# Differential attention heads: two softmax maps combined by the ratio of their sums

## The chip, the cores and the metric

The kernel runs on one core of a Trainium2 chip. The time is the device time of one execution in microseconds (us); before the change the median of three runs is 2071.48 us (2070.87 to 2072.05). The core's engines are called PE (TensorE, matrix products), DVE (VectorE), ACT (ScalarE), POOL (GpSimd) and SP (SyncE, which here only issues DMAs). Each works through its own queue in order and waits on the others by semaphores.

## The reference

One layer of an encoder on a sequence of 16 + 1024 tokens, width 1024, all in float32: a SwiGLU block, a mixing block and a second SwiGLU block, each added to the stream h, and a last norm. In the mixing block the normed stream is projected once, and its columns go to two groups of heads. Four differential heads attend to everything, four pairs of heads of width 64 in a sliding window. The differential part, cut to what is computed:

```python
s = einsum('bqhcd,bkhcd->bhcqk', q, k) * scale      # c = 0, 1: two maps per head
p = softmax(s, axis=-1)
a = p[:, :, 0] - lam * p[:, :, 1]                   # lam: a learned number
o = einsum('bhqk,bkhe->bqhe', a, v)                 # e = 128
o = rmsnorm(o, sub_gain) * (1.0 - lambda_init)      # over e, per head and query; EPS = 1e-6
```

`rmsnorm(x, g)` is `x * rsqrt(mean(x * x) + EPS) * g`. The outputs of both groups go through `w_out` and are added to h.

## The kernel before, in words

The activations lie transposed, features on the 128 partitions and tokens along the row. Large products are made of three float32r products, of a high and a low half of each operand (`split`: ACT casts the high half, DVE or POOL subtracts it for the low one). The kernel is scheduled as a whole: `TileContext(nc, schedule_with_timeline_sim=True)` takes the program's instructions and sets the order of each engine's queue itself, and memory is reused between pools (`Rings`, one pool for each buffer of a ring), with waits where a new buffer lies on an old one. So any edit may change the order in places that it doesn't touch.

The stages by time in the span: the first SwiGLU block, 0 to about 720 us; the projections, 720 to about 1040, with the window attention mixed into their later part; the differential heads, about 1044 to 1320; the second SwiGLU block, to about 1900; the last products and the norm.

Where the projections begin, the first block's last product (`pd`, L167 called from `down_last`) ends, the stream's chunks are normed (`norm_chunk`: `nsq` and `nacc` the squares and their sum, `nps` the sum over partitions on PE, `ns`, `nr` the root, `ny` the normed chunk on DVE L149, `u_hi`, `u_lo` its halves) and `proj_t` (L806) multiplies them with one tile of the input weights after the other. `load_w` loads such a tile into `pwraw` (one buffer), casts `pwhi` on ACT and subtracts `pwlo` on DVE for the first tile, kb, and on POOL for the second, qb. `pj` are the products, `z` what is copied out of them. Behind them `pv` multiplies with the value weights (`wvraw`, `wv_hi`, `wv_lo`).

A differential head has 8 tiles of 128 queries, so there are 32 maps in all. For each, `scores` (L773) makes two score tiles `ds` of 128x1040 on PE (component 0 and 1), DVE takes their row minimum `dmx` (L784; the scores carry a minus sign), and ACT the exponential into `dp0` and `dp1` (L786), with the sum of each row in `z[:, 0]` and `z[:, 1]`, 128x2. `combine` (L789) makes the map of the head: DVE inverts both sums (`drz`), POOL multiplies the second map by its inverse sum and by `neglam` (minus lambda, L793), DVE multiplies the first by its inverse sum and adds (L794). The map is then transposed on PE in blocks of 128x128 (`dt`, L1167, L1175) and copied to `at` by DVE (L1170) and ACT (L1172, L1176); `values` multiplies with v (L1183, `do`) and ACT copies to `oh` (L1186).

The loop over maps works with a lead: at step i the scores of map i, the combine of map i - 1, the transposes of map i - 2 and the values of the pair before. Three maps of the first head are computed early, while the window attention ends (`EARLY`). When a head has four maps, `head_norm` (L1131) squares `oh` on ACT, sums over the partitions by a product with `ones` on PE (`sums`, L1082), takes the root (`rsqrt`, L1095: ACT's table root and one step of refinement on DVE) and scales on POOL (L1122). The next head's keys and queries are loaded and split during the head before (`load_head`, L745; `kl` and the low half of `qst` on POOL, L114 and L760; `kraw` and `qraw` have one buffer each). In the first head the norm of the window part (`win_norm`) uses the same engines, and product tiles of the output weights for it (`out_win`) fill PE's gaps from map 9 on.

Of the kernel before, what the change touches and what calls it, by code (L numbers as in the profile page):

```python
# [10 lines left out]
F32 = mybir.dt.float32  # L11
# [40 lines left out]
def layer(  # L52
# [50 lines left out]
    nc.vector.tensor_scalar(dgain, dgain, -0.5 / P * (1.0 - LAMBDA_INIT), None, op0=ALU.mult)  # L103

    neglam = cpool.tile([P, 1], F32, name="neglam")

    h_d = dpool.tile([D, L], F32, name="h_d")

# [4 lines left out]
    def tt(eng, out, a, b, op):  # L113
        eng.tensor_tensor(out, a, b, op=op)  # L114
# [671 lines left out]
        nc.scalar.activation(p, full, AF.Exp, bias=mx, scale=-1.0, accum_out=z[:, c : c + 1])  # L786
        ps_p.append(p)

    def combine(ps_p, z):  # L789
        rz = dp.tile([P, 2], F32, tag="drz", name="drz")  # L790
        nc.vector.reciprocal(rz, z)
        p0, p1 = ps_p
        nc.gpsimd.tensor_scalar(p1, p1, rz[:, 1:2], neglam, op0=ALU.mult, op1=ALU.mult)  # L793
        nc.vector.scalar_tensor_tensor(p0, p0, rz[:, 0:1], p1, op0=ALU.mult, op1=ALU.add)  # L794
        return p0

    pend, sc = {}, {}
# [1 line left out]
    with ExitStack() as st:  # L799
# [236 lines left out]
        for i, (kv, n) in enumerate(units):  # L1036
# [18 lines left out]
            if i in EARLY:  # L1055
                for t in EARLY[i]:
                    sc[t] = score_tiles()
                    for c in range(2):
                        scores(heads[0], t, c, sc[t], ds0)
                    pend[t] = combine(*sc.pop(t))  # L1060
            if n == NB - 1 and kv == 0:
                for g in range(4):
                    qs[1, g] = win_q(4 + g)
# [9 lines left out]
    with ExitStack() as st:  # L1073
# [5 lines left out]
        ow_hi = op.tile([P, 4, SEQ], F32R, name="ow_hi")  # L1079
        ow_lo = op.tile([P, 4, SEQ], F32R, name="ow_lo")  # L1080

        def sums(srcs, n):  # L1082
            acc = npool.tile([P, 512], F32, tag="nacc", name="nacc")[:, :n]
            for i, s in enumerate(srcs):
                if i == 0:
                    nc.scalar.activation(acc, s, AF.Square)
                else:
                    sq = npool.tile([P, 512], F32, tag="nsq", name="nsq")[:, :n]
                    nc.scalar.activation(sq, s, AF.Square)
                    nc.gpsimd.tensor_tensor(acc, acc, sq, op=ALU.add)  # L1090
            ps = psum.tile([P, 512], F32, tag="do", name="do")[:, :n]
            nc.tensor.matmul(ps, ones, acc, start=True, stop=True)
            return ps

        def rsqrt(v, n, width):  # L1095
            r = npool.tile([P, SEQ], F32, tag="nr", name="nr")[:, :n]
            nc.scalar.activation(r, v, AF.Abs_reciprocal_sqrt, bias=eps, scale=1.0 / width)
            for c0 in range(0, n, 512):
                vc, rc = v[:, c0 : c0 + 512], r[:, c0 : c0 + 512]
                t = npool.tile([P, 512], F32, tag="nt", name="nt")  # L1100
                nc.scalar.activation(t, rc, AF.Square)
                nc.vector.scalar_tensor_tensor(t, vc, EPS * width, t, op0=ALU.add, op1=ALU.mult)
                nc.vector.scalar_tensor_tensor(rc, t, -3.0 * width, rc, op0=ALU.add, op1=ALU.mult)
            return r

# [24 lines left out]

        def head_norm(hd, c, oh):  # L1131
            os = [oh[:, c0 : c0 + n] for c0, n in CH_REAL]
            ps = sums([os[c]], 512)
            if hd == 3:
                head_scale(hd, c, os[c], rsqrt(ps, 512, P))
                return
            if c == 0:
                nvs[hd] = npool.tile([P, SEQ], F32, tag="nv", name="nv")
            nc.scalar.copy(nvs[hd][:, c * 512 : (c + 1) * 512], ps)
            if c == 1:  # L1140
                r = rsqrt(nvs[hd], SEQ, P)
                for j in range(2):
                    head_scale(hd, j, os[j], r[:, j * 512 : (j + 1) * 512])

# [53 lines left out]
        for i in range(NQ + 4):  # L1198
# [6 lines left out]

            def do_combine():
                if N_EARLY < i <= NQ:
                    pend[i - 1] = combine(*sc.pop(i - 1))

            def do_t():  # L1210
                next(tg, None)
# [204 lines left out]
```

## Time and profile before

| | |
|---|---|
| median of the runs | 2071.48 us (2070.87 to 2072.05) |
| the profiled execution's own time | 2074.79 us |
| its span | 2072.9 us |
| mean granted clock of PE | 0.981 of 2.4 GHz |
| PE busy | 1943.9 us, 94% |
| DVE busy | 1279.3 us, 62% |
| ACT busy | 879.4 us, 42% |
| POOL busy | 960.3 us, 46% |

The profile is of one execution; its span runs from the first to the last instruction. Busy time of PE is counted with a pipelined instruction's overlap left out, and a PE at half clock counts as busy too, so busy time and the granted clock are read together.

### The profile page before, as it was taken

The page shows a single profiled execution, that of the slowest core. Times are in us where ns is not written, and L with a number is a line of the kernel's source. Part 1 is how long each engine was busy: PE and PEld are TensorE (multiplying, and loading weights), DVE is VectorE, ACT ScalarE, POOL GpSimd, SP SyncE. Part 2 cuts the span into 40 slices and gives each one's busy share as a digit, 9 for nine tenths or more (in the row PEclk, how much of TensorE's full clock was granted, in tenths as well). Part 3 has the DMA queues.
Part 4 walks back from the last instruction along what each step waited for, and adds up shares of the span by engine and source line. Part 5 has one row for each costly group of instructions (what it writes and reads, how often), then busy time and mean ns, then how long its engine had stood idle before and what let it go on. Part 6 is the DMA issues. An engine that isn't in the chain of part 4 may idle for free.

```text
span 2072.9 us, 30356 instructions
## 1 busy us (share of the span) xinstructions
PE 1943.9 (94%) x11484; PEld 1692.1 (82%) x11484; DVE 1279.3 (62%) x1853; ACT 879.4 (42%) x1611; POOL 960.3 (46%) x807
## 2 busy tenths in 40 slices
PE   5999999998999989899978999898999999989998
PEld 4999999998999879777756777676778888877877
DVE  7855554548875660376766777477665555487745
ACT  6433333334432431366566666354333333344433
POOL 0565454545443740576456432003655554454443
PEclk9999999999999999999988999999999999999999
DMA  5332322328422351544442321622323223375122
GB/s 172 108 109 98 120 92 97 109 92 319 155 64 81 133 174 52 143 122 123 105 113 67 97 85 39 203 102 81 124 106 122 95 89 117 130 282 167 61 82 82
DMA packets 106003, 244.14 MB, mean 118 GB/s; under 512 B 14209, under 2 KB 29009, under 8 KB 105857
## 3 DMA queue, kind: packets, MB, share of 16 engines
q1 hardware_dynamic: 94336, 204.53, 31.1%
q0 software_dynamic: 11520, 37.67, 4.6%
q8 instruction: 90, 1.47, 0.3%
q14 instruction: 57, 0.46, 0.1%
HBM read 169.86 MB, written 65.44 MB: 114 GB/s over the span
## 4 chain that ended last, share of the span: by engine, by line
PE 70%; DVE 11%; DMA 6%; ACT 5%; POOL 3%; issue 3%; SPq 1%; DVEq 0%; POOLq 0%; ACTq 0%
PE p L226 35%; PE pA L577 7%; PE pj L167 5%; PE pC L577 3%; PE pv L884 3%; PE pd L167 2%; PE ds L780 2%; DVE bl L114 2%; PE po L167 2%; PE do L1183 2%; PE pB L577 2%; PE do L167 1%; DMA ru<-wu 1%; POOL s L114 1%; ACT dp L786 1%
## 5 line engine op out<-in xcount | busy, mean ns | idle before, releaser
L114 POOL TENSOR_TENSOR s<-ru 128x512 f32<-128x512 f32 x42 | 55.9, 1331 | 264.5 <-DMA ru<-wu 190.1
L226 PE MATMUL p<-b_hi,wal 128*128 128x260 f32 (+1 forms) x528 | 141.5, 323 | 5.7 <-DVE wal L114 5.7
L226 PE MATMUL p<-b_hi,wah 128*128 128x260 f32 (+1 forms) x528 | 143.2, 325 | 3.6 <-ACT wah L117 1.6
L226 PE MATMUL p<-t_hi,wch 128*128 128x260 f32 (+1 forms) x528 | 141.2, 321 | 5.7 <-DVE u L114 5.7
L226 PE MATMUL p<-b_lo,wah 128*128 128x260 f32 (+1 forms) x528 | 142.5, 322 | 3.4 <-DVE b_lo L114 3.4
L226 PE MATMUL p<-t_lo,wch 128*128 128x260 f32 (+1 forms) x528 | 141.0, 321 | 0.0
L226 PE MATMUL p<-t_hi,wcl 128*128 128x260 f32 (+1 forms) x528 | 140.8, 321 | 0.0
L226 PE MATMUL p<-t_lo,wbh 128*128 128x260 f32 (+1 forms) x504 | 135.5, 319 | 0.0
L226 PE MATMUL p<-t_hi,wbl 128*128 128x260 f32 (+1 forms) x504 | 133.4, 320 | 0.0
L226 PE MATMUL p<-t_hi,wbh 128*128 128x260 f32 (+1 forms) x504 | 133.1, 320 | 0.0
L114 DVE TENSOR_TENSOR u<-p,m 128x520 f32<-128x520 f32 (+1 forms) x88 | 61.0, 693 | 116.5 <-PE p L226 108.9
L117 ACT CAST wbh<-s 128x512 fp32r<-128x512 f32 x84 | 52.1, 621 | 164.9 <-PE p L226 142.1
L577 PE MATMUL pA<-bh,wh 128*128 128x260 f32 (+1 forms) x432 | 115.3, 322 | 2.6 <-DVE h L584 2.6
L577 PE MATMUL pA<-bl,wh 128*128 128x260 f32 (+1 forms) x432 | 114.7, 319 | 0.0
L117 ACT CAST wah<-rg 128x512 fp32r<-128x512 f32 x88 | 53.9, 620 | 143.0 <-PE p L226 112.1
L577 PE MATMUL pA<-bh,wl 128*128 128x260 f32 (+1 forms) x432 | 111.9, 319 | 1.8 <-POOL wl L114 1.8
L114 DVE TENSOR_TENSOR wal<-rg,wah 128x512 fp32r<-128x512 f32 x88 | 74.0, 847 | 63.6 <-ACT wah L117 63.6
L114 DVE TENSOR_TENSOR bl<-r,bh 128x520 fp32r<-128x520 f32 (+1 forms) x126 | 109.0, 900 | 3.3 <-ACT bh L117 2.6
L117 ACT CAST wch<-ru 128x512 fp32r<-128x512 f32 x88 | 54.7, 621 | 130.5 <-PE p L226 72.6
L584 DVE SCALAR_TENSOR_TENSOR h<-pA,h 128x520 f32<-128x520 f32 (+1 forms) x96 | 66.1, 690 | 63.2 <-PE pA L577 63.1
L117 ACT CAST wh<-s 128x384 fp32r<-128x384 f32 x96 | 49.1, 513 | 130.1 <-PE pA L577 65.5
L114 POOL TENSOR_TENSOR s<-wr 128x384 f32<-128x384 f32 x48 | 55.4, 1157 | 100.6 <-DVE wl L114 89.7
(290 smaller groups left out, 6113.2 us busy)
## 6 DMA issues: line engine op xcount, KB each, us to landing
rg<-wg SPq DMA_DIRECT2D x44, 512.0 KB, 3.6
ru<-wu SPq DMA_DIRECT2D x44, 512.0 KB, 5.0
wr<-wd SPq DMA_DIRECT2D x24, 768.0 KB, 4.4
r<-g_t SPq DMA_DIRECT2D x12, 780.0 KB, 5.8
r<-g_t SPq DMA_DIRECT2D x12, 768.0 KB, 5.3
g_b<-g POOLq DMA_DIRECT2D x27, 260.0 KB, 5.2
r<-g_b SPq DMA_DIRECT2D x9, 780.0 KB, 6.4
g_b<-g POOLq DMA_DIRECT2D x27, 256.0 KB, 5.1
```

Source lines behind the costliest of these rows:

```text
L114: eng.tensor_tensor(out, a, b, op=op)
L117: nc.scalar.copy(hi, src)
L167: nc.tensor.matmul(o, w, x[:, c0 : c0 + n], start=first and i == 0, stop=last and i == 2)
L226: nc.tensor.matmul(o, w_k(ww, k), x[:, k, c0 : c0 + cn], start=first and k == 0 and i == 0, stop=k == hk - 1 and i == 2, skip_group_check= ...
L577: nc.tensor.matmul(o, w_k(ww, k), xx[:, c0 : c0 + cn], start=new and k == 0 and q == 0, stop=k == DNG - 1 and q == 2, skip_group_check=not ...
L584: nc.vector.scalar_tensor_tensor(hs, full, 0.5, hs, op0=ALU.mult, op1=ALU.add)
L780: nc.tensor.matmul(o, qs[c][:, qt * P : (qt + 1) * P], kk[:, c0 : c0 + n], start=i == 0, stop=i == 1)
L786: nc.scalar.activation(p, full, AF.Exp, bias=mx, scale=-1.0, accum_out=z[:, c : c + 1])
L884: nc.tensor.matmul(ps[:m, 192 + c * 320 : 512 + c * 320], u[:, k, sl], w[:, k, c * 320 : (c + 1) * 320], start=k == 0 and i == 0, stop=k = ...
L1183: nc.tensor.matmul(po[:, :256], v[:m, j, :], at[:m, j, :], start=j == 0, stop=j == NB)
```

## The change

Softmax's first sum z0 is a factor of a whole row of the combined map, and the norm behind it divides by the row's size anyway. After the change the map stays unnormalised, p0 + p1 * (neglam * z0 / z1), which is z0 times the map of before. The ratio takes two small DVE instructions, a reciprocal of z1 and a scalar_tensor_tensor, both 128x1; one DVE pass of 128x1040 combines, and POOL's pass is gone. The norm's mean of squares is now z0 squared times too large, so its epsilon is multiplied by z0 squared: `combine` stores z0 * z0 of each map in a column of `zsq`, and `sums`, for a head, adds to each block of 128 queries of the squares the diagonal matrix `ident_eps` (EPS * 128 on the diagonal) times that column, four DVE passes of 128x128 for each call, so that the product with `ones` adds it to every row. `rsqrt` then has no epsilon of its own there. `zero`, `zsq` and `ident_eps` are new constants, 644 bytes on each partition, which are allocated ahead of everything else.

```diff
     neglam = cpool.tile([P, 1], F32, name="neglam")
+    zero = cpool.tile([P, 1], F32, name="zero")
+    nc.vector.memset(zero, 0.0)
+    zsq = cpool.tile([P, 4 * NB], F32, name="zsq")
+    ident_eps = cpool.tile([P, P], F32, name="ident_eps")
+    nc.vector.tensor_scalar(ident_eps, ident, EPS * P, None, op0=ALU.mult)
...
-    def combine(ps_p, z):
-        rz = dp.tile([P, 2], F32, tag="drz", name="drz")
-        nc.vector.reciprocal(rz, z)
+    def combine(t, ps_p, z):
+
+        rz = dp.tile([P, 1], F32, tag="drz", name="drz")
+        nc.vector.reciprocal(rz, z[:, 1:2])
+        nc.vector.scalar_tensor_tensor(rz, z[:, 0:1], neglam, rz, op0=ALU.mult, op1=ALU.mult)
         p0, p1 = ps_p
-        nc.gpsimd.tensor_scalar(p1, p1, rz[:, 1:2], neglam, op0=ALU.mult, op1=ALU.mult)
-        nc.vector.scalar_tensor_tensor(p0, p0, rz[:, 0:1], p1, op0=ALU.mult, op1=ALU.add)
+        nc.vector.scalar_tensor_tensor(p0, p1, rz, p0, op0=ALU.mult, op1=ALU.add)
+        tt(nc.vector, zsq[:, t : t + 1], z[:, 0:1], z[:, 0:1], ALU.mult)
         return p0
...
-        def sums(srcs, n):
+        def sums(srcs, n, zs=None):
...
+            for j in range(n // P if zs is not None else 0):
+                aj = acc[:, j * P : (j + 1) * P]
+                nc.vector.scalar_tensor_tensor(aj, ident_eps, zs[:, j : j + 1], aj, op0=ALU.mult, op1=ALU.add)
             ps = psum.tile([P, 512], F32, tag="do", name="do")[:, :n]
             nc.tensor.matmul(ps, ones, acc, start=True, stop=True)
             return ps
 
-        def rsqrt(v, n, width):
+        def rsqrt(v, n, width, e=EPS):
             r = npool.tile([P, SEQ], F32, tag="nr", name="nr")[:, :n]
-            nc.scalar.activation(r, v, AF.Abs_reciprocal_sqrt, bias=eps, scale=1.0 / width)
+            nc.scalar.activation(r, v, AF.Abs_reciprocal_sqrt, bias=eps if e else zero, scale=1.0 / width)
...
-                nc.vector.scalar_tensor_tensor(t, vc, EPS * width, t, op0=ALU.add, op1=ALU.mult)
+                nc.vector.scalar_tensor_tensor(t, vc, e * width, t, op0=ALU.add, op1=ALU.mult)
...
-            ps = sums([os[c]], 512)
+            ps = sums([os[c]], 512, zsq[:, hd * NB + c * 4 : hd * NB + c * 4 + 4])
             if hd == 3:
-                head_scale(hd, c, os[c], rsqrt(ps, 512, P))
+                head_scale(hd, c, os[c], rsqrt(ps, 512, P, 0.0))
```

The scheduler's order changes with it. DVE, where the projections begin: before, the low half of the first projection weight is subtracted ahead of the first block's last operands (`glo`), and waits for its load and for ACT.

```order
L584 SCALAR_TENSOR_TENSOR h_5808<-pA,h_5808 128x520 [waits PE_49]
L114 TENSOR_TENSOR pwlo<-pwraw,pwhi 128x1024 [waits DMAHW6_49,Activation_49]
L584 SCALAR_TENSOR_TENSOR h_5812<-pB,h_5812 128x520 [waits PE_49]
L584 SCALAR_TENSOR_TENSOR h_5808<-pA,h_5808 128x520 [waits PE_49]
L114 TENSOR_TENSOR glo<-graw,ghi 128x1040 [waits DMAHW2_49,Activation_49]
```

After, the same instruction (L119 there) stands some 45 rows further on, in the norm of the second chunk.

```order
L147 SCALAR_TENSOR_TENSOR nr<-ns,nr 128x264 [waits DVE_49]
L154 SCALAR_TENSOR_TENSOR ny<-h_5841,gains,nr 128x264 [waits DVE_49,Pool_49]
L154 SCALAR_TENSOR_TENSOR ny<-h_5833,gains,nr 128x264
L154 SCALAR_TENSOR_TENSOR ny<-h_5825,gains,nr 128x264 [waits Pool_49]
L646 SCALAR_TENSOR_TENSOR h_5821<-pd,h_5821 128x264 [waits PE_49]
L119 TENSOR_TENSOR pwlo<-pwraw,pwhi 128x1024 [waits DMAHW6_49,PE_49]
```

It now waits for PE, and has moved behind the root of the second chunk, three `ny` and an `h`. PE's third projection product, which reads it, has a wait for DVE that it didn't have before.

SP, same place: before, the load of the second projection weight (the second `pwraw` here) stands among the loads of the first block's last operands.

```order
L621 DMA wdraw<-wd 128x512
L175 DMA pwraw<-win 128x1024 [waits DMAHW6_49,PE_49]
L621 DMA wdraw<-wd 128x512 [waits DMAHW3_49,Pool_49]
L621 DMA wdraw<-wd 128x512 [waits DMAHW5_49,DMAHW0_49,Pool_49]
L614 DMA graw<-g_d_102 128x1040 [waits DMAHW1_49,DMASW1_49,DMAHW4_49,DMASW0_49,Pool_49]
L175 DMA pwraw<-win 128x1024 [waits DMAHW6_49,DMAHW2_49,DVE_49]
```

After, it is the first `pwraw` of this piece; the second is the third weight's.

```order
L727 DMA h_d<-h_5821 128x264 [waits DMAHW7_49,DVE_49]
L1161 DMA hrm<-h_d 128x512 [waits DMAHW0_49,PE_49,Activation_49]
L180 DMA pwraw<-win 128x1024 [waits DMAHW1_49,DVE_49]
L1161 DMA hrm<-h_d 128x512 [waits DMAHW2_49]
L727 DMA h_d<-h_5813 128x264 [waits DMAHW3_49,DVE_49]
L180 DMA pwraw<-win 128x1024 [waits DMAHW4_49,DMAHW1_49,Pool_49]
L878 DMA wvraw<-wv 128x640 [waits DMAHW5_49]
```

It has moved behind the stores of h and waits for DVE, which reads the one buffer; the third weight's load, ahead of the value weights, waits for POOL.

POOL, in the first head, where the second head's keys and queries are split: before, the passes of L793 stand in this chain.

```order
L114 TENSOR_TENSOR kl<-kraw,kh 128x1040 [waits DMAHW0_49,DMAHW1_49,PE_49,Activation_49]
L793 TENSOR_SCALAR dp_13143<-dp_13143,drz,neglam 128x1040 [waits DVE_49,Pool_49]
L760 TENSOR_TENSOR qst<-qraw,qst 64x1024 [waits DMAHW4_49,Activation_49,Pool_49]
L793 TENSOR_SCALAR dp_13196<-dp_13196,drz,neglam 128x1040 [waits DVE_49,Pool_49]
L1090 TENSOR_TENSOR nacc<-nacc,nsq 128x512 [waits PE_49,Activation_49]
L114 TENSOR_TENSOR kl<-kraw,kh 128x1040 [waits DMAHW7_49,DMAHW6_49,Activation_49]
```

After:

```order
L119 TENSOR_TENSOR kl<-kraw,kh 128x1040 [waits DMAHW0_49,DMAHW7_49,PE_49,Activation_49]
L765 TENSOR_TENSOR qst<-qraw,qst 64x1024 [waits DMAHW2_49,Activation_49,Pool_49]
L1097 TENSOR_TENSOR nacc<-nacc,nsq 128x512 [waits PE_49,Activation_49,Pool_49]
L119 TENSOR_TENSOR kl<-kraw,kh 128x1040 [waits DMAHW7_49,DMAHW6_49,Activation_49]
L1097 TENSOR_TENSOR nacc<-nacc,nsq 128x512 [waits Activation_49]
```

The query's split follows the key's at once; the rest of the chain keeps its order.

## Rows read from the trace of the kernel before

**Rows 1.** The page: busy time by engine, and the chain that ended last.

```profile
PE 1943.9 (94%) x11484; PEld 1692.1 (82%) x11484; DVE 1279.3 (62%) x1853; ACT 879.4 (42%) x1611; POOL 960.3 (46%) x807
...
PE 70%; DVE 11%; DMA 6%; ACT 5%; POOL 3%; issue 3%; SPq 1%; DVEq 0%; POOLq 0%; ACTq 0%
```

**Rows 2.** Stage windows: length, busy us (instructions) of each engine, PE clock, DMA, GB/s.

```profile
core 0: us, PE busy (x) PEld busy (x) DVE busy (x) ACT busy (x) POOL busy (x), PEclk, DMA share, GB/s
1060.00:1140.00 80.00, 61.35 (x267) 47.62 (x268) 53.35 (x60) 53.12 (x91) 44.16 (x29) 0.81 0.24 67
1140.00:1280.00 140.00, 132.02 (x705) 106.33 (x704) 104.23 (x123) 92.35 (x163) 53.73 (x36) 1.00 0.26 78
```

**Rows 3.** PE's waits, 1140 to 1300: total us, times, longest.

```profile
PE ds L780 <- ACT dp L786: 5.7, 9, 0.9
PE dt L1167 <- ACT at L1176: 5.2, 7, 1.1
```

**Rows 4.** Groups by line, 1044 to 1320: busy us, mean ns | idle before, releaser.

```profile
L794 DVE SCALAR_TENSOR_TENSOR dp<-dp,drz,dp 128x1040 f32<-128x1040 f32 x32 | 43.7, 1365 | 3.4 <-POOL dp L793 3.1
...
L793 POOL TENSOR_SCALAR dp<-dp,drz,neglam 128x1040 f32<-128x1040 f32 x32 | 40.9, 1277 | 75.3 <-DVE drz L791 74.8
...
L1097 ACT ACT_TABLE_LOAD x6 | 7.7, 1283 | 0.1
...
L791 DVE RECIPROCAL drz<-dz 128x2 f32<-128x2 f32 x32 | 5.1, 161 | 18.1 <-ACT dp L786 18.1
```

**Rows 5.** Two single lines of DVE: duration ns min/median/max, when, forms.

```profile
L916 DVE TENSOR_TENSOR neglam<-lsum x1: 160/160/160, 839.2 to 839.2; 128x1 f32<-128x1 f32 x1
...
L913 DVE TENSOR_TENSOR lprod<-lamt x1: 293/293/293, 838.3 to 838.3; 128x128 f32<-128x128 f32 x1
```

**Rows 6.** Timeline of the last head: start us, us, engine, line, instruction [idle before].

```profile
1297.43 1.29 DVE L794 SCALAR_TENSOR_TENSOR dp<-dp,drz,dp 128x1040 f32<-128x1040 f32 x1
...
1307.80 0.66 PE L1167 MATMUL dt<-ident,dp 128*128 128x128 f32 x4 [0.34 <-ACT at L1176]
```

**Rows 7.** Timeline of the projections' start.

```profile
723.25 0.40 PE L167 MATMUL pj<-u_hi,pwlo 128*128 128x512 f32 x1
...
723.92 4.26 DVE L149 SCALAR_TENSOR_TENSOR ny<-h,gains,nr 128x264 f32<-128x264 f32 x3
...
724.40 2.59 POOL L114 TENSOR_TENSOR pwlo<-pwraw,pwhi 128x1024 fp32r<-128x1024 f32 x1
...
726.76 0.40 PE L167 MATMUL pj<-u_hi,pwlo 128*128 128x512 f32 x1
...
728.11 0.42 DVE L641 SCALAR_TENSOR_TENSOR h<-pd,h 128x264 f32<-128x264 f32 x1
...
729.69 1.29 DVE L149 SCALAR_TENSOR_TENSOR ny<-h,gains,nr 128x264 f32<-128x264 f32 x3
...
748.03 1.22 DVE L114 TENSOR_TENSOR pwlo<-pwraw,pwhi 128x1024 fp32r<-128x1024 f32 x1 [2.23 <-ACT pwhi L117]
...
748.99 0.73 PE L167 MATMUL pj<-u_hi,pwhi 128*128 128x512 f32 x2 [1.73 <-ACT z L829]
...
768.66 1.44 PE L884 MATMUL pv<-wv_hi,u_hi 128*128 128x320 f32 x4 [2.99 <-ACT wv_hi L117]
```

**Rows 8.** Timeline of the first head.

```profile
1106.30 1.24 POOL L793 TENSOR_SCALAR dp<-dp,drz,neglam 128x1040 f32<-128x1040 f32 x1
...
1112.46 2.30 DVE L794 SCALAR_TENSOR_TENSOR dp<-dp,drz,dp 128x1040 f32<-128x1040 f32 x1 [1.83 <-POOL dp L793]
...
1116.03 1.04 ACT L759 CAST qst<-qraw 128x1024 fp32r<-128x1024 f32 x1 [1.71 <-DMA qraw<-qa_d]
...
1117.29 1.11 PE L1167 MATMUL dt<-ident,dp 128*128 128x128 f32 x4 [3.08 <-ACT at L1176]
```

**Rows 9.** Window of 8 us around that wait's end, columns as in rows 2.

```profile
1116.00:1124.00 8.00, 6.53 (x22) 4.93 (x22) 2.75 (x4) 4.33 (x9) 7.06 (x5) 0.57 0.53 131
```

**Rows 10.** DMA issues: engine, times, KB each, median us to landing.

```profile
pwraw<-win SPq DMA_DIRECT2D x13, 512.0 KB, 4.5
```

More of the change, by code (lines that the diff above doesn't have):

```diff
@@ L1059, in layer @@
                         scores(heads[0], t, c, sc[t], ds0)
-                    pend[t] = combine(*sc.pop(t))
+                    pend[t] = combine(t, *sc.pop(t))
             if n == NB - 1 and kv == 0:
@@ L1140, in head_norm @@
             if c == 1:
-                r = rsqrt(nvs[hd], SEQ, P)
+                r = rsqrt(nvs[hd], SEQ, P, 0.0)
                 for j in range(2):
@@ L1207, in do_combine @@
                 if N_EARLY < i <= NQ:
-                    pend[i - 1] = combine(*sc.pop(i - 1))
+                    pend[i - 1] = combine(i - 1, *sc.pop(i - 1))
             def do_t():
```

## The prediction

> **What bounds the kernel now.** I read the page's totals first: PE is busy 94% of the span and makes up 70% of the chain that ended last, against 11% for DVE and 3% for POOL [rows 1]. So the change pays only where PE stands still, or runs at half clock, for want of a combined map. Second, the stage windows, to find such places. The differential stage has two halves. In its first head, 1060 to 1140 us, PE is busy 61.35 of 80 us at a granted clock of 0.81; in the steady heads, 1140 to 1280, it is busy 132.02 of 140 at 1.00, and 8.0 us are idle [rows 2]. Third, the waits of PE in the steady heads: none names POOL or the combine; the two large ones are for the exponentials, 5.7 us in 9 waits, and for copies of transposed maps on ACT, 5.2 us in 7 [rows 3]. Last, the timelines of the two places where the order moves: the start of the projections (720 to 770 us) and the first head.
>
> **What the change removes.** 32 POOL passes over 128x1040, mean 1277 ns, and with them the hand-over from POOL to DVE, for which DVE waited 3.1 us in all; the DVE pass behind them keeps its shape, mean 1365 ns [rows 4]. POOL is at 46% and no PE wait of the steady heads is for it, so the 40.9 us themselves are worth nothing.
>
> **What it adds.** Per map on DVE: one 128x1 scalar_tensor_tensor and one 128x1 product, each priced by the 128x1 product at 160 ns, and, as 32 stand in the program for 32 maps, one 128x128 epsilon step, priced by the 128x128 product at 293 ns [rows 5]. The reciprocal gets one column instead of two, at its 161 ns [rows 4]. Sum: 2 x 0.160 + 0.293 = 0.613 us per map, 19.6 us for 32. None of these shapes with a scalar operand from a tile stands in the trace of before; the nearest rows are those two, and from below the bound is nothing where DVE has its idle time. In the steady heads DVE is busy 104.23 of 140 us [rows 2]; some 20 of the 32 maps pass there, so it goes to 116 of 140. From exponential to combined map the path even shortens, by 1.21 for POOL less 0.16 for the ratio; but as PE works two maps behind the scores, nobody waits there. What can come through is a later minimum on DVE, then a later exponential, for which PE does wait. Bounds for the three steady heads: 24 x 0.613 = +14.7 if all of it delays PE, and -5.2 if the waits for copies go. Nearest the rows is almost nothing, as a quarter of DVE is idle: I take +1.5.
>
> In the last head ACT loads its tables twice more, 1283 ns each [rows 4], since the norm's root is put ahead of the last exponential. The last map is combined at 1297.43 + 1.29 = 1298.7, and PE transposes it at 1307.80 [rows 6]: 9.1 us of cover. The two loads, the root and its copy put it off by some 4 us, so the cost is 0, and it would show only if the cover fell under that.
>
> **What the order moves: the start of the projections.** This is the dearest part, and the diff doesn't show it. The low half of the first projection weight (pwlo of kb) was split on DVE long before use; now it stands behind three ny and an h of the norm, since it waits for PE. Before, PE's third projection product, the first that reads it, ran at 723.25 with no wait; three ny begin at 723.92 [rows 7]. At the earliest pwlo now ends at 723.92 + 1.29 (three ny, alone) + 0.42 (h) + 1.22 (a pwlo, alone) = 726.85, which is 3.6 late. At the latest, with the ny as long as they were (4.26) and pwlo as long as on POOL (2.59): 731.19, 7.9 late [rows 7]. What made the three ny 4.26 instead of 1.29 was the other weight's pwlo on POOL from 724.40, and this has moved behind; nacc and u_lo of POOL still stand beside it. I take +5.5, near the middle.
>
> The Trainium skill ("SBUF — State Buffer", section "Who interferes with whom") says that a VectorE instruction with two SBUF inputs and a GpSimd one that reads SBUF exclude each other for a whole instruction. The trace agrees: the excess of 2.97 is even above the 2.59 of the POOL pass beside it. By that rule pwlo, which has two such inputs, waits for what POOL has begun, and the step goes to the 7.9; without it 3.6.
>
> Behind a stall the clock falls: after PE's 3.08 us wait in the first head the granted clock is 0.57 for 8 us, with 6.53 us of PE busy [rows 8, 9], which at full clock would be 3.7; so up to +2.8 more. I take +2. Given back: PE's 1.73 wait for z at 748.99 [rows 7], because kb's last products now come before 24 of the next tile and not right ahead of its successor: -1.7. The second weight is loaded only when the first has been read, say 728.7: its 4.5 us of landing [rows 10] and 2.59 on POOL, with a cast between for which I allow 1, give 736.8. PE meanwhile has 22 products at (726.76 - 723.25)/15 = 0.234 us [rows 7], 5.1, the norm's sums and 16 short ones, some 2.5: 736.3. That is +0.5, with 0 to 2 as bounds. Later PE waits 2.99 for wv_hi [rows 7]; those loads are now queued on SP behind a load that waits for POOL's pwlo, so they slip as well: I count 1 back, bounds 0 to 3. Sum of the place: 5.5 + 2 - 1.7 + 0.5 - 1 = +5.3, from 0 (3.6 - 1.7 + 0 + 0 - 3 and rounded up, since a stall this long hardly vanishes) to +11 (7.9 + 2.8 - 1.7 + 2).
>
> **What the order moves: the first head.** POOL's chain there is key split, map pass, query split, and the query's buffer is single: the pass of 1.24 at 1106.30 stands ahead of the query split, whose end lets the next query load start; ACT waits 1.71 for that load at 1116.03, and PE 3.08 for a copy behind it on ACT; DVE waits 1.83 for POOL and then needs 2.30 instead of 1.29 [rows 8, 4]. In the new order no map pass stands in this chain. The load comes at least 1.24 earlier, at most the whole 3.08 goes: -2.2. The half clock behind it is worth up to 2.8: -2. DVE's 1.83 + 1.01 reaches PE through minimum and exponential, in half I suppose, and other heads of the chain give a little: -1.8. Sum -6. Bounds: the 18.65 us that PE is idle in these 80 [rows 2] from below; +3 from above, if the transposes of the window part, which also change places with the scores, leave one more gap like the 3.08.
>
> The starts of both FFN stages keep their instructions; a few change places at the second, at no price that a row gives: 0, give or take 2.
>
> **Sum.** +5.3 - 6 + 1.5 + 0 = +0.8. On the profiled execution's own 2074.79 that is 2075.6; this one lay 3.3 above the median of the runs shown, 2071.48, and so I forecast 2072 for the median.
>
> **The rivals.**
> 1. Faster: the first head's gaps mostly close, since POOL's and DVE's queues both get lighter there. For it: PE idle 18.65, the clock of 0.81. Against it: most of PE's waits there are for exponentials, whose number is the same. Two thirds of the idle time, -12.4, and with the clock -2.8; with +5.3 at the projections and +1.5: -8.4, that is 2063.
> 2. Slower: the late pwlo stops PE at the projections' start and nothing is given back. Place: PE's third projection product, near 723. It decides once pwlo ends after 729, that is with more than 5.7 of stall: 7.9 + 2.8 - 1.7 + 2 = +11; with the first head at -3 and steady heads at +1.5: +9.5, that is 2081. For it: the wait is now a true dependency, and PE has nothing else in its queue. Against it: the POOL pass that made the ny long has moved away.
> 3. Slower: DVE becomes the bound of the steady heads, at 83% busy. Half of the 14.7 comes through: +7.4, in place of the 1.5: +6.7, that is 2078. Against it: DVE's work is spread evenly, and the longest wait for an exponential is 0.9.
> 4. The change does what it says and both places cost or give under 2 us: 2071 to 2072, told apart from my forecast only by the trace.
>
> **How the numbers follow.** Less than 0.2% (4.1 us) can't be told from no change here. My forecast and rival 4 together: 0.40; rival 1: 0.29; rival 2: 0.22; rival 3: 0.09. Some of rivals 2 and 3 would end within 0.2% and some of my own case outside it, which evens out: faster 0.29, same 0.39, slower 0.32. The likeliest case's own range is 2067.5 to 2076; reaching to rival 1 and rival 2, the range is 2062 to 2083.
>
> **What would show it.** Right at the projections: PE's third product there begins 4 to 8 us after the first, released by DVE's pwlo, with a clock near 0.6 behind it. Right in the first head: PE busy over 61.35 of 80 us or the stretch shorter, no wait of 3 us for a copy. Right in the steady heads: each at most 2 us longer than before, DVE busy 80 to 85%. Wrong: a stage that is longer with its PE waits on DVE's minimum, the norm's sums on PE waiting for the epsilon steps, or a stretch of the FFN that differs by more than 2 us.

## The result: 51 us slower

The changed kernel takes 2122.67 us (2121.17 to 2126.46) against 2071.77 us for the kernel before on the same chip (2070.87 to 2076.78): ratio 1.024, 95% interval 1.0225 to 1.0256. The forecast was 2072 with a range from 2062 to 2083; the time lies 40 us above its end, and no rival came near it.

The page of the changed kernel, busy time and chain, answers to [rows 1]:

```profile
PE 1964.2 (93%) x11484; PEld 1704.3 (80%) x11484; DVE 1296.8 (61%) x1951; ACT 883.0 (42%) x1613; POOL 913.1 (43%) x775
...
PE 73%; DVE 9%; DMA 5%; ACT 5%; POOL 3%; issue 3%; SPq 1%; DVEq 0%; POOLq 0%; ACTq 0%
```

Totals tell little here: DVE has gained 17.5 us, POOL has lost 47.2, PE has the same 11484 products. The profiled span has grown by 48.7 us, so I cut both spans at instructions that both kernels have: the first projection product `pj`, the first score product `ds`, the first product `po` of the output weights with the differential heads, and the start of the last group of `pd` products.

| part | before | after | difference |
|---|---|---|---|
| start to the first `pj` (first feed-forward block) | 722.7 | 728.1 | +5.4 |
| first `pj` to the first `ds` (projections, window attention) | 321.8 | 318.2 | -3.6 |
| first `ds` to the first `po` (differential heads: "the stage" below) | 273.5 | 312.6 | +39.1 |
| first `po` to the last `pd` group (second feed-forward block) | 743.2 | 751.0 | +7.8 |
| rest | 11.7 | 11.7 | 0 |

The stage has four fifths of it. As a whole, before and then after, with the columns of [rows 2]:

```profile
1044.50:1317.90 273.40, 238.05 (x1188) 186.15 (x1186) 185.18 (x217) 173.62 (x303) 116.92 (x76) 0.94 0.29 85
```

```profile
1046.30:1358.90 312.60, 251.36 (x1193) 194.54 (x1191) 212.50 (x314) 176.09 (x306) 74.69 (x46) 0.90 0.26 75
```

PE stands idle 25.9 us longer, and is busy 13.3 us longer with the same products, while the mean granted clock falls from 0.94 to 0.90. In the first head nothing is lost: from the first `ds` to the fourth norm product (`do<-nacc,ones`) it is 107.7 us before and 106.8 after. All of the rest is in the steady heads. Windows of half heads (four maps), each from one norm product to the next, of the kernel before:

```profile
1152.20:1179.00 26.80, 23.91 (x123) 18.18 (x122) 19.61 (x24) 19.11 (x32) 10.18 (x8) 1.00 0.12 41
1179.00:1208.50 29.50, 28.65 (x157) 23.59 (x156) 20.39 (x23) 17.76 (x34) 12.98 (x9) 1.00 0.51 135
...
1237.00:1266.00 29.00, 28.20 (x157) 23.42 (x157) 20.16 (x23) 15.84 (x32) 8.00 (x7) 1.00 0.23 73
```

and of the kernel after; the first line is the first head's window of [rows 2]:

```profile
1060.00:1140.00 80.00, 58.84 (x279) 45.52 (x278) 58.23 (x85) 53.14 (x90) 27.48 (x16) 0.87 0.27 73
...
1153.00:1190.00 37.00, 28.13 (x139) 22.05 (x139) 28.51 (x40) 22.04 (x38) 9.29 (x6) 0.93 0.12 36
1190.00:1224.00 34.00, 31.94 (x152) 25.41 (x153) 22.54 (x36) 16.65 (x31) 5.12 (x3) 0.87 0.44 117
1224.00:1264.00 40.00, 29.50 (x140) 23.11 (x140) 28.51 (x39) 22.36 (x39) 9.56 (x6) 0.91 0.10 33
1264.00:1298.00 34.00, 31.77 (x159) 25.37 (x160) 23.81 (x38) 15.93 (x31) 0.50 (x1) 0.91 0.19 63
```

There are two patterns. The six half heads behind the fourth norm product took 27.0, 29.4, 28.8, 29.0, 28.8 and 23.5 us; they take 37.2, 33.8, 40.4, 33.5, 32.8 and 28.7. So each is at least 4 us longer, and the first and the third another 6 to 7; and a clock that was 1.00 throughout is now near 0.9. DVE, 71% busy over the four windows (103.37 of 145 us), isn't the bound. PE's waits, 1140 to 1330, answer to [rows 3]:

```profile
PE do L1102 <- DVE hrm L119: 12.6, 5, 5.1
PE ds L785 <- ACT dp L791: 7.2, 8, 2.5
PE dt L1177 <- ACT at L1186: 6.4, 10, 2.2
```

The first is new: the norm's product waits for DVE, in two of five times by 5.1 us. Groups by line, ACT's exponential and then DVE's, answering to [rows 4, 5]:

```profile
L791 ACT ACTIVATE dp<-ds,dmx 128x1040 f32<-128x1040 f32 x64 | 71.6, 1119 | 16.5 <-DVE dmx L789 12.9 <-DVE zsq L119 2.1 <-DVE drz L798 1.4
L800 DVE SCALAR_TENSOR_TENSOR dp<-dp,drz,dp 128x1040 f32<-128x1040 f32 x32 | 42.6, 1330 | 0.8
L1100 DVE SCALAR_TENSOR_TENSOR nacc<-ident_eps,zsq,nacc 128x128 f32<-128x128 f32 x32 | 19.5, 667 | 4.6 <-ACT nacc L1093 4.6
...
L798 DVE SCALAR_TENSOR_TENSOR drz<-dz,neglam,drz 128x1 f32<-128x1 f32 x32 | 8.6, 268 | 35.6 <-ACT dp L791 35.5
L119 DVE TENSOR_TENSOR zsq<-dz 128x1 f32<-128x1 f32 x32 | 7.8, 242 | 5.3 <-ACT dp L791 5.2
```

The combine's pass is as long as before. The epsilon step L1100 has a mean of 667 ns, 2.3 times the 293 that I gave it. The timeline of one group of four shows why:

```profile
1182.89 2.43 POOL L119 TENSOR_TENSOR kl<-kraw,kh 128x1040 fp32r<-128x1040 f32 x1 [10.55 <-ACT kh L122]
1183.14 6.35 DVE L1100 SCALAR_TENSOR_TENSOR nacc<-ident_eps,zsq,nacc 128x128 f32<-128x128 f32 x4
...
1185.41 2.34 POOL L765 TENSOR_TENSOR qst<-qraw,qst 64x1024 fp32r<-64x1024 f32 x1
1187.82 1.26 POOL L119 TENSOR_TENSOR owlo<-owraw,owhi 128x512 fp32r<-128x512 f32 x1
1189.42 0.68 DVE L119 TENSOR_TENSOR hrm<-do,hrm 128x512 f32<-128x512 f32 x1
1190.24 2.05 PE L1102 MATMUL do<-nacc,ones 128*128 128x512 f32 x2 [5.09 <-DVE hrm L119]
```

Four steps that take 1.1 us together in six of the eight groups take 6.35 here, and again at 1257: they get by one at a time, as POOL's three passes end. PE's next instruction is the norm's product, which needs them and the bank that `hrm`, queued on DVE behind them, empties. The clock pays as well, in the windows behind that wait (length, PE busy, granted clock, DMA share, GB/s):

```profile
1190.00:1194.00 4.00, 3.15 (x8) 0.50 0.71 197
1194.00:1198.00 4.00, 4.00 (x17) 0.50 1.01 244
```

The 4 us of every half head look different. PE after, from a stretch where no group is held:

```profile
1296.84 0.60 PE L1177 MATMUL dt<-ident,dp 128*128 128x128 f32 x4
1297.87 1.10 PE L1102 MATMUL do<-nacc,ones 128*128 128x512 f32 x2 [0.44 <-DVE hrm L119]
1298.81 0.27 PE L1185 MATMUL dt<-ident,dp 128*16 128x128 f32 x1
1299.79 0.66 PE L1177 MATMUL dt<-ident,dp 128*128 128x128 f32 x4 [0.71 <-ACT at L1186]
1300.90 0.74 PE L785 MATMUL ds<-kh,qst 128*128 128x264 f32 x3 [0.46 <-ACT dp L791]
...
1303.84 0.70 PE L1177 MATMUL dt<-ident,dp 128*128 128x128 f32 x4 [1.72 <-ACT at L1182]
```

and before, in the same place of a half head:

```profile
1262.01 0.60 PE L1167 MATMUL dt<-ident,dp 128*128 128x128 f32 x4
...
1265.21 0.27 PE L1175 MATMUL dt<-ident,dp 128*16 128x128 f32 x1
...
1266.27 1.02 PE L1092 MATMUL do<-nacc,ones 128*128 128x512 f32 x2
```

Before, twelve output products (2.8 us; left out at the first "...") stand between a map's second group of transposes and its tail of 16 columns, while ACT copies that group out of the only `dt` bank. After, these twelve stand ahead of the second group; group, norm product, tail and next group follow each other, and PE waits between them: 0.44 for `hrm`, 0.71 for the copy of the tail, 0.46 for an exponential and 1.72 for the copy of the group before, 3.3 us in all. That last copy comes late because ACT does the norm's root ahead of it:

```profile
1300.87 1.28 ACT L1107 ACT_TABLE_LOAD   x1
1302.16 1.15 ACT L1107 ACTIVATE nr<-nv,zero 128x1024 f32<-128x1024 f32 x1
1303.22 0.56 ACT L1182 COPY at<-dt 128x512 f32<-128x512 f32 x1
```

Before, the root stood on ACT too, from 1269.54 to 1271.98, and PE waited for no copy there. I had taken the steady heads' order for unchanged; it is not.

### The profile page after: what moved, and what is told of

It reads as the page before. It is cut to its first block, busy times and chain, and to the rows that moved or that the text cites. A ratio compares the mean times of both kernels' runs of the same rounds, so it can differ in the third digit from the quotient of the medians.

```text
span 2121.6 us, 30457 instructions
## 1 busy us (share of the span) xinstructions
PE 1964.2 (93%) x11484; PEld 1704.3 (80%) x11484; DVE 1296.8 (61%) x1951; ACT 883.0 (42%) x1613; POOL 913.1 (43%) x775
## 4 chain that ended last, share of the span: by engine, by line
PE 73%; DVE 9%; DMA 5%; ACT 5%; POOL 3%; issue 3%; SPq 1%; DVEq 0%; POOLq 0%; ACTq 0%
PE p L231 37%; PE pA L582 8%; PE pC L582 4%; PE pj L172 4%; PE ds L785 3%; PE do L1193 3%; PE pv L891 3%; PE pd L172 2%; PE po L172 2%; PE pB L582 2%; DVE bl L119 2%; PE do L172 1%; PE dt L1177 1%; ACT dp L791 1%; PE wo L1024 1%
## 5 line engine op out<-in xcount | busy, mean ns | idle before, releaser
L119 POOL TENSOR_TENSOR s<-ru 128x512 f32<-128x512 f32 x42 | 55.2, 1315 | 254.9 <-DMA ru<-wu 186.9
L119 DVE TENSOR_TENSOR u<-p,m 128x520 f32<-128x520 f32 (+1 forms) x88 | 60.9, 692 | 119.8 <-PE p L231 114.0
L119 DVE TENSOR_TENSOR bl<-r,bh 128x520 fp32r<-128x520 f32 (+1 forms) x126 | 110.1, 908 | 4.2 <-ACT bh L122 3.7
L231 PEld LDWEIGHTS p<-t_hi,wch 128*128 128x128 f32 x528 | 87.3, 188 | 16.0 <-DVE u L119 7.8
L231 PEld LDWEIGHTS p<-b_hi,wah 128*128 128x128 f32 x528 | 88.6, 191 | 13.8 <-ACT wah L122 2.1
```

Source lines behind the costliest of these rows:

```text
L231: nc.tensor.matmul(o, w_k(ww, k), x[:, k, c0 : c0 + cn], start=first and k == 0 and i == 0, stop=k == hk - 1 and i == 2, skip_group_check= ...
```

## The experiments

All times are medians, and the ratio is to the kernel before, timed beside it. The three last columns are cut as in the table above, from one profiled execution each; as the kernel before alone runs in 2065 to 2079 us, differences of a few us there tell little. Before they are 273.5, 321.8 and 743.2, after 312.6, 318.2 and 751.0. Each expectation weighs theories against each other, and the text behind it uses their names.

| kernel | median, us | ratio, 95% interval | stage | first `pj` to first `ds` | second block |
|---|---|---|---|---|---|
| no_eps | 2096.38 | 1.0118 (1.0098 to 1.0138) | 291.6 | 318.5 | 749.0 |
| consts_only | 2078.67 | 1.0031 (1.0014 to 1.0049) | 271.9 | 316.3 | 748.2 |
| eps_only | 2097.21 | 1.0120 (1.0097 to 1.0144) | 292.4 | 317.9 | 750.8 |
| eps_product | 2108.60 | 1.0178 (1.0157 to 1.0198) | 303.8 | 316.2 | 750.2 |
| no_eps_dz4 | 2099.66 | 1.0127 (1.0102 to 1.0152) | 291.3 | 318.0 | 748.5 |
| no_eps_no_zsq | 2104.23 | 1.0144 (1.0120 to 1.0168) | 289.5 | 319.1 | 753.9 |
| no_eps_pool | 2078.85 | 1.0032 (1.0016 to 1.0049) | 273.7 | 316.5 | 750.5 |
| load_early | 2119.92 | 1.0221 (1.0199 to 1.0243) | 316.1 | 317.7 | 747.9 |
| no_eps_order | 2084.83 | 1.0067 (1.0046 to 1.0088) | 278.8 | 317.2 | 750.6 |
| consts_rev | 2107.35 | 1.0183 (1.0157 to 1.0210) | 296.5 | 316.9 | 750.9 |
| after_order | 2103.47 | 1.0161 (1.0137 to 1.0184) | 297.1 | 316.6 | 754.7 |
| eps_one_input | 2073.61 | 1.0007 (0.9995 to 1.0020) | 269.9 | 314.8 | 748.1 |
| diag_order | 2105.81 | 1.0157 (1.0131 to 1.0184) | 303.3 | 322.0 | 744.9 |
| diag | 2120.70 | 1.0228 (1.0198 to 1.0259) | 319.5 | 316.6 | 744.4 |
| no_eps_order_no_zsq | 2088.37 | 1.0074 (1.0045 to 1.0103) | 282.1 | 316.6 | 751.6 |

**Which part of the change.** no_eps takes the epsilon loop out of `sums` (and leaves the norm's epsilon out); consts_only is the kernel before with the constants alone; eps_only is the kernel before with the constants and the loop, which there adds zeros.

```diff
-            for j in range(n // P if zs is not None else 0):
-                aj = acc[:, j * P : (j + 1) * P]
-                nc.vector.scalar_tensor_tensor(aj, ident_eps, zs[:, j : j + 1], aj, op0=ALU.mult, op1=ALU.add)
```

> The changed kernel without the four epsilon steps of each head sum (the norm's epsilon is left out); the combine on VectorE, the constants and their memory stay. Theory 1 (the epsilon steps in front of the norm's product hold TensorE, twice behind GpSimd's splits of the next keys and queries, 6.35 and about 6 us instead of 1.1): the stage from the first scores to the first output product falls from 312.6 to about 272 to 280 us, total 2080 to 2090. Theory 2 (the combine's added VectorE instructions delay the exponentials): the stage stays above 300, total above 2108. Theory 3 (the constants' memory reorders the program): no effect here, total 2115 to 2125.

> The kernel before with only the three new constants (644 bytes per partition, set and not read). Theory 3 (memory and order alone): total 2095 or more. Theories 1 and 2: only the projections' start (late low half of the first weight) and the feed-forward stages change, 2068 to 2084; TensorE's third projection product begins 4 to 8 us after the first.

> The kernel before with the constants and the epsilon steps (they add zero, as the column of sums is set to 0 and the norm keeps its own epsilon), combine as before with GpSimd's pass. Theory 1: total 2105 to 2125, epsilon steps that meet GpSimd's splits take 4 to 6.5 us for four, TensorE waits about 5 us for them at these places. Theory 2: total below 2085.

Neither of theories 1 and 2 stands alone: no_eps and eps_only both lie between their numbers. Above the 271.9 of consts_only, the combine costs 19.7 us (no_eps), the epsilon steps 20.5 (eps_only), and both together 40.7 (after). That they add up so well is in part chance: in eps_only the order has changed too. Of its last twelve tiles of twelve output products, three stand ahead of the second transposes, as they do after; in consts_only none does. Theory 3 falls for the stage, but the constants cost by themselves 0.3% (0.14 to 0.49%).

**The epsilon steps.** eps_product writes them to a tile of their own, with a second product:

```diff
-                nc.vector.scalar_tensor_tensor(aj, ident_eps, zs[:, j : j + 1], aj, op0=ALU.mult, op1=ALU.add)
+                    nc.vector.tensor_scalar(ez[:, j * P : (j + 1) * P], ident_eps, zs[:, j : j + 1], None, op0=ALU.mult)
...
+                nc.tensor.matmul(ps, ones, ez, start=False, stop=True)
```

> The changed kernel with the epsilon steps written to a tile of their own (identity times column, one input from SBUF) and added by a second product with ones on TensorE, 8 products of 128x512 more (about 0.6 us each). Theory 1: the steps no longer meet GpSimd, each about 0.3 us also beside it, the waits of 5 us go; total 2080 to 2095. Theory 2: above 2108.

Theory 1 missed. The time is over theory 2's 2108 by 0.6 us, but for another reason: the eight extra products take 1.02 us each, 8.2 us in all, and the steps still meet POOL, though they have one input:

```profile
1190.93 2.70 POOL L765 TENSOR_TENSOR qst<-qraw,qst 64x1024 fp32r<-64x1024 f32 x1 [0.68 <-ACT qst L764]
1191.27 2.44 DVE L1102 TENSOR_SCALAR nsq<-ident_eps,zsq 128x128 f32<-128x128 f32 x1
```

load_early should have moved POOL's splits away (`i % NB == 2` for `i % NB == 4` at `load_head`).

> The changed kernel with the next head's keys and queries loaded at the third map of a head instead of the fifth. Theory 1 (epsilon steps that meet GpSimd's splits): if the splits move away from the epsilon steps all eight groups take 1.1 us and the two halves of a head that took 37 and 40 us take 33; total 2103 to 2110. If contention isn't the cost, 2118 to 2126 with groups of 1.1 us. If the groups still meet, the run tells only that those that do are the long ones.

It is the third case: the groups met the splits as before (6.35 us at both places), and the run tells nothing more. eps_one_input is eps_only with the steps in another form, at the same place and of the same size; each leaves two instructions, the pass and a read of its row sum (78 to 91 ns):

```diff
-                nc.vector.scalar_tensor_tensor(aj, ident_eps, zs[:, j : j + 1], aj, op0=ALU.mult, op1=ALU.add)
+                nc.vector.tensor_scalar(aj, aj, zs[:, j : j + 1], 0.0, op0=ALU.add, op1=ALU.add, accum_out=zero)
```

> The kernel before with the constants, and in the place of each epsilon step a tensor_scalar that adds a zero to the same 128x128 block, in place, with one input from SBUF and a row sum written out: as many VectorE instructions at the same place, without a second input. Theory 1a (two inputs from SBUF make the step wait for GpSimd's whole passes): all groups of four take 1 to 1.6 us also beside GpSimd, the longest half head falls from 36.7 to about 31, the stage from 292.4 to 282 to 287. Theory 1b (any VectorE instruction beside GpSimd is held): groups of 4 us or more remain, the stage stays at 290 to 294.

The stage is 269.9, far better than the 282 to 287 of theory 1a, and the time is that of the kernel before. One group in the midst of POOL's split, eps_only first, then eps_one_input:

```profile
1241.03 2.44 POOL L120 TENSOR_TENSOR kl<-kraw,kh 128x1040 fp32r<-128x1040 f32 x1 [1.91 <-ACT kh L123]
1241.52 6.12 DVE L1099 SCALAR_TENSOR_TENSOR nacc<-ident_eps,zsq,nacc 128x128 f32<-128x128 f32 x4
```

```profile
1168.51 2.44 POOL L120 TENSOR_TENSOR kl<-kraw,kh 128x1040 fp32r<-128x1040 f32 x1 [1.92 <-ACT kh L123]
1169.00 0.34 DVE L1099 TENSOR_SCALAR_CACHE_REDUCE nacc<-nacc,zsq 128x128 f32<-128x128 f32 x1
...
1170.16 0.35 DVE L1099 TENSOR_SCALAR_CACHE_REDUCE nacc<-nacc,zsq 128x128 f32<-128x128 f32 x1
```

So with this form the steps cost nothing, at the same place and with more instructions: what costs is the meeting with POOL. The 20.5 us of eps_only are not all theirs, since its order had partly changed and that of eps_one_input has not (one tile of twelve). With the order asked for on both sides (after_order against no_eps_order, below) the steps cost 18.3 us (18.6 in the medians): PE is idle 10.8 us longer and busy 7.4 longer at a mean clock of 0.92 for 0.95. The form that isn't held adds one number to each partition, and the epsilon needs a diagonal; no run has a diagonal that isn't held.

**The combine.** Four tries on no_eps: more buffers for sums and ratio, no square of the first sum, POOL's pass back, and the order.

> The changed kernel without epsilon steps (the norm's epsilon is left out), with four buffers instead of two for the sums and for the ratio. Theory A (the sums' buffer is now held until the ratio and the square have been read, so the exponential two maps on waits for VectorE): the stage from first scores to first output product falls from 291.6 to 275 to 280 us, total about 2082. Theory B (without GpSimd's pass the scheduler puts TensorE's second group of transposes behind the twelve output products, so that the copies' latency lies bare; buffers don't matter): the stage stays at 288 to 293, total 2092 to 2098.

> As the one without epsilon steps, and the square of the first sum is not computed either (32 small VectorE products less, 7.8 us). Theory C (the number of small VectorE instructions delays the minima): the stage falls by half of its excess or more, to 283 or less. Theory B: 286 to 292, since the order of TensorE is the same.

> As the one without epsilon steps, but GpSimd multiplies the second map by the ratio and VectorE adds the maps (the square and the ratio stay on VectorE). One instruction more for each map, and the hand-over is back. Theory B: the transposes stand ahead of the twelve output products again, the stage falls to 272 to 277 us, total 2075 to 2084. Theories A and C: the stage stays above 288, as small instructions and buffers are the same.

```diff
-        nc.vector.scalar_tensor_tensor(p0, p1, rz, p0, op0=ALU.mult, op1=ALU.add)
+        nc.gpsimd.tensor_scalar(p1, p1, rz, 1.0, op0=ALU.mult, op1=ALU.mult)
+        tt(nc.vector, p0, p0, p1, ALU.add)
```

Buffers (291.3) and the square (289.5) don't matter; theories A and C fall. With POOL's pass back the stage is 273.7, though each map has one instruction more than in no_eps and two more than before; in that kernel the scheduler puts the twelve output products behind the second transposes again. To part the order from the work, the order alone was changed, both ways. no_eps_order asks for the old one; `issue_after` queues what its block issues behind the instruction that it is given:

```diff
+            before_fill = last_t[0]
             for z in range(3):
                 do_t()
                 if z < 2:
-                    do_w()
+                    if work is fill and before_fill is not None:
+                        with tc.issue_after(before_fill.ins):
+                            do_w()
+                    else:
+                        do_w()
```

consts_rev gives the kernel with constants alone the new one (the output products of the next step are issued ahead of the second transposes, which are queued behind them with the same `issue_after`), and after_order is the full change with the old order.

> The changed kernel without epsilon steps (the norm's epsilon is left out), with the twelve output products of a step queued on TensorE behind the second group of transposes of the map before, as the scheduler had it in the kernel before; nothing else is asked. Theory B (the place of these products in TensorE's queue is the cost): the stage from first scores to first output product falls from 291.6 to 270 to 277 us, total 2072 to 2084. Theory D (VectorE's added work itself is the cost, the order only goes with it): the stage stays above 285, total above 2090.

> The kernel before with the new constants and with the reverse order: the second group of transposes of a map queued behind the twelve output products that stood behind it; combine as before, by GpSimd and VectorE, no epsilon steps. Theory B: the stage grows from 271.9 to 285 to 293, total 2090 to 2100. Theory D: it stays at 270 to 276, total 2074 to 2082.

> The full change, with the output products queued behind the transposes as in the one above it. Theory B: 18 of the 39 us of the stage go, total 2100 to 2106, what stays is the epsilon steps' part, above all where they meet GpSimd's splits (groups of 4 to 6.5 us). Theory D: total above 2115.

Theory B holds in both directions: the new order costs consts_only 24.6 us (271.9 to 296.5, more than the 293 expected), the old order gives 12.8 back to the combine (291.6 to 278.8) and 15.5 to the full change (312.6 to 297.1). PE's waits from 1152 on, consts_only and then consts_rev, the same work in the two orders:

```profile
PE dt L1173 <- ACT at L1182: 5.6, 8, 1.1
PE ds L786 <- ACT dp L792: 4.0, 7, 0.8
```

```profile
PE dt L1176 <- ACT at L1181: 7.0, 4, 2.9
PE dt L1176 <- ACT at L1185: 6.1, 11, 1.2
```

The transposes' waits for copies more than double, and the longest is 2.9 us, as in no_eps. Of the 7.0 us in four waits, 6.3 are three waits (1.7, 1.7, 2.9) for a copy that stands on ACT behind the norm's root and its table loads, as at 1303 above. But 7 us of the combine stay (278.8 against 271.9), a third of its 19.7 for theory D. Were they VectorE's small instructions?

> The changed kernel without epsilon steps and without the square of the first sum (the norm's epsilon is left out), output products queued behind the transposes. It tells whether the 7 us that stay above the stage of the kernel with constants alone (278.8 against 271.9) are VectorE's small instructions: if so 272 to 275 us, total 2074 to 2080; if they are the pass itself or the order's rest 277 to 280, total 2082 to 2087.

At 282.1, above even the 280 expected, it isn't the square. In the steady heads of no_eps_order PE waits 6.2 us in eight waits for DVE's copy of transposes, 0.8 in one in consts_only; in seven of the eight the combine's pass has gone ahead of that copy on DVE. That points at VectorE's pass, which no longer waits for POOL's and so comes earlier; no run parts it from what the order still has different.

So the stage's way from 271.9 to 312.6 is, by these runs: 6.9 us for the combine in the old order, 18.3 for the epsilon steps, 15.5 for the order.

**A combine without epsilon.** Dividing by z0 in the transposes needs no change to the norm and no constants: POOL writes `ident` times 1/z0, and TensorE multiplies by it.

```diff
-                    nc.tensor.transpose(pt[:, j * P : (j + 1) * P], a[:, kk * P : (kk + 1) * P], ident)
+                    last_t[0] = nc.tensor.matmul(
+                        pt[:, j * P : (j + 1) * P], a[:, kk * P : (kk + 1) * P], dg, start=True, stop=True
+                    )
```

> The kernel before with the maps combined by the ratio in one VectorE pass and the row's first sum divided out in the transposes: GpSimd writes the identity times 1/z0 (128x128, one input), and TensorE multiplies the map by it instead of by the identity, so that nothing is added to the norm and no constants are needed; output products queued behind the second transposes of the map before. Theories so far (order, and the epsilon steps' second input, are the cost; 32 passes of GpSimd less are worth little): stage 270 to 278 us against 273.5, feed-forward and projections as before since the memory is, total 2066 to 2078. If a pass of VectorE in the place of GpSimd's costs by itself: 280 or more, total above 2080.

> As the one with the identity times 1/z0, with the order that the scheduler gives. Theory B (it puts the output products ahead of the transposes again): stage 285 to 296, total 2085 to 2095. If the order is no matter: as the one with the order asked for.

Both are slower than the kernel before and missed their numbers, for a reason that I hadn't priced: a float32 product by a matrix is issued twice where the transpose was once. The same blocks are x256 and 41.7 us in the kernel before, and in diag

```profile
L1173 PE MATMUL dt<-ddg,dp 128*128 128x128 f32 x512 | 73.9, 290 | 12.0 <-ACT at L1184 6.5 <-DVE at L1178 2.4 <-POOL ddg L795 1.9
```

which is 32 us more of PE. They still serve as tests: the order alone is again worth 16.2 us (319.5 against 303.3), and without the constants the second block takes 744.4 and 744.9 us, as before (743.2), where the thirteen others, all with constants, and the changed kernel, take 747.9 to 754.7. So the 5 to 8 us there go with the constants; by what wait is not shown.

No version beat the kernel before; eps_one_input, which only adds zeros to it, equals it.

## Why the prediction was wrong, step by step

In the prediction's own terms the profiled spans differ by -3.6 at the projections (+5.3 forecast), -0.9 in the first head (-6), +40 in the steady heads (+1.5) and +13.2 in the two feed-forward blocks (0).

- **The steady heads, "I take +1.5"** is the step that failed; it was +40. Even its bound, +14.7, was for the wrong mechanism, a later minimum on DVE: ACT's wait for the minimum fell, from 16.5 to 12.9 us. What came in its place are the two next points, the held epsilon steps (18.3 us) and the order of the output products (15.5), with some 7 us of the combine. DVE's added work was 667 + 268 + 242 ns a map for my 613, 37.7 us for 19.6, of which 10.4 is in the two held groups. The prediction had named the right sign, "the norm's sums on PE waiting for the epsilon steps", but given it no price.
- **The epsilon step at 293 ns.** Alone it takes 344 (median). I priced it beside nothing, though its place, just ahead of a product that PE waits for and at the time of POOL's splits, could be read from the order. Beside POOL the step with two inputs from SBUF was held up to 2495 ns, the plain tensor_scalar of eps_product up to 2437, and the form that also writes its row sum took at most 348. The Trainium skill ("SBUF — State Buffer", section "Who interferes with whom") says that a VectorE instruction with two SBUF inputs contends with a GpSimd one that reads SBUF, that tensor_scalar can contend too, and that its form which writes out the accumulator does not; the three measurements agree. I had weighed this at the projections and not here.
- **The order of the output products.** I compared the order at three places and took the steady heads' for unchanged. Without a POOL pass that nobody waited for, the scheduler gave another order, and that moved 2.8 us of cover away from a copy; why it did so is not shown. This is 13 to 25 us, the runs' range. No run shows a gain from taking the pass away, as forecast. The last half head, where I counted "9.1 us of cover" and a cost of 0, is 5.2 us longer, with the stage's longest wait for a copy of transposes (2.9 us); consts_rev has a wait of 2.9 too, so it goes with the order.
- **The projections, "+5.3".** The mechanism was right, its end wrong. After:

```profile
729.34 2.08 DVE L154 SCALAR_TENSOR_TENSOR ny<-h,gains,nr 128x264 f32<-128x264 f32 x3
...
731.68 1.67 DVE L119 TENSOR_TENSOR pwlo<-pwraw,pwhi 128x1024 fp32r<-128x1024 f32 x1
733.41 0.80 PE L172 MATMUL pj<-u_hi,pwlo 128*128 128x512 f32 x1 [4.58 <-DVE pwlo L119]
```

  The third product begins 5.3 us after the first, with the clock at 0.50 from 733 to 737. But the waits for z and wv_hi of [rows 7], 1.73 and 2.99, are gone, and up to 780 us one of 1.35 is all that the later products have. The part up to the first scores is even 3.6 us shorter, and rival 2 falls. The stall (4.57 to 4.59 us) is in all fourteen kernels with the constants, consts_only among them, and in none of the three without, so it goes with the constants and not with the combine. What made the part shorter isn't shown; diag, without constants or stall, has 316.6 there.
- **The first head, "-6".** POOL's chain is lighter (27.48 us busy of 80 for 44.16), the clock 0.87 for 0.81; the head gained 0.9. That POOL's pass in the query's chain was what cost there had been argued, and taking it out didn't give the 6 us.
- **The feed-forward blocks, "0, give or take 2".** The second is +7.8, with 5 of it in consts_only. The first is +5.4, of which consts_only shows 4.1 (726.8 for 722.7); other runs lie between 721.9 and 726.4, so little can be made of it.
- **The range** took its ends from the rows of before. None of them could show an epsilon step beside POOL, and the price of a lone 128x128 product stood for it.

## What to carry to other kernels

Price an added VectorE instruction with what GpSimd does at that moment, above all where TensorE's next instruction waits for it: the same four steps cost 1.1 or 6.35 us. Where a scheduler sets the order, compare for every steady loop what stands between a TensorE group and the one that needs its bank; an instruction that nobody waits for can, by leaving, move the work that covered a copy. And constants that a change allocates ahead of everything can be felt in stages that it doesn't touch: 0.3% here.

## What the runs showed of the hardware that I had not expected

Of VectorE's forms on a 128x128 float32 block beside a GpSimd pass of 2.4 us: scalar_tensor_tensor with two inputs from SBUF up to 2495 ns after and 2532 in eps_only (344 and 346 in the median), plain tensor_scalar up to 2437 (281), tensor_scalar with a row sum 322 to 348 beside it or not. A float32 product of 128x128 by a diagonal costs TensorE two issues of 290 ns, its transpose one of 288.
